# Hybrid Fourier / state-space encoder layer on one core: modulation matmuls turned round and half of them moved, weight sums queued behind weight loads, one norm moved into the MLP

## Chip, cores and metric

One core of a Trainium2 chip runs the whole layer as one program. The metric is the device time of one execution in microseconds; the lower, the better. Everything is computed in 32-bit floats.

## The reference, cut to what matters

One encoder layer for two requests (2048 and 512 tokens of width 1024; here side by side as 2560 tokens, features on the partitions).

```python
mod = silu(c) @ w_ada + b_ada                  # 1024 -> 6*1024, one row for each request
shift1, scale1, gate1, shift2, scale2, gate2 = split(mod, 6)
h  = rmsnorm(x, g_mix_norm) * (1 + scale1) + shift1
z  = h @ w_in
yf = fourier_mixer(z[..., :512])               # 2-D DFT, then a map for each head
ys = s5_mixer(z[..., 512:])                    # complex diagonal state space, both directions, GELU, GLU
x  = x + gate1 * (concat(rmsnorm(yf), rmsnorm(ys)) @ w_out)
h  = rmsnorm(x, g_mlp_norm) * (1 + scale2) + shift2
x  = x + gate2 * (square(relu(h @ w_mlp_in + b_in)) @ w_mlp_out + b_out)
y  = rmsnorm(x, g_final)
```

## The kernel before, in words

The program is straight-line code. A scheduler in the framework orders the instructions of each engine and each DMA queue when the program is built: an instruction is placed when it is ready in the scheduler's model, and of several that are ready the one written first goes first. At run time every engine and every queue keeps that order. SyncE (SP) only issues DMAs; ScalarE (ACT) and GpSimd (POOL) issue some between their own instructions. Most matmuls multiply split operands: `mm3` (L228 to 231) does three products, high by high, high by low, low by high, one pass each in fp32r. Plain fp32 matmuls take two records each in the trace.

Four stages follow each other, with some overlap.

1. **Input projection** (`mix_in`, to about 340 us). `ada1` makes the first 16 of the 48 modulation blocks of 128 columns (`mod[:, 0:16]`, shift1 and scale1) with the weights as the moving operand, 512 columns at a time (L705), then turns the result round with small transposes (L710). Beside the projection `zs` of five token tiles, `ssm_pre` (from about 55 to 177 us) builds the input and shift matrices of the state space, 8 groups `q`, at a raised priority and with its own three PSUM banks (`self.side = True`, L882). After each group it calls `ada_slot` twice (L290), but in the kernel before `ada_open(pre, A1)` with `A1 = 16` leaves these calls with nothing to do.
2. **State space beside Fourier mixing** (from about 340 to 690 us). For 8 groups `q`, `Ssm.lead` (psV matmuls, L350), `step1`, `step2`, `step3` (V sweeps on DVE, L403 to 417; psY matmuls, L382). Between these steps `slot` (L959) does one modulation block and one unit of the Fourier generator (`fourier`, then `out_f`, whose matmuls are `pof`). There are 32 such slots, two in each of the first two and last two rounds of the loop and four in each of the six between, so the 32 modulation blocks 16 to 47 are spread over the stage. A block is `ada(j)` (L681): eight fp32 matmuls with a 128x128 piece of the weights as the stationary operand and the two columns of `cs` as the moving one, then one DVE add (L688). Its weights (512 KB) are loaded by SP two blocks ahead (`AB = 2` buffers).
3. **Second half of the mixer** (`mix_out`, from about 690 to 1050 us). For five blocks `b` of 512 tokens: `gelu`, `glu`, and `out`, the output projection with the residual (`pout`), which stores the new x to `x1D`, sums its squares into `ss`, makes the row scales with `rbc` (matmuls `pn` L736, a power on POOL L750, matmuls `pb` L754, a copy on ACT L755) and stores them to `rD`. The MLP uses a Strassen-like scheme with seven products, for which sums of the weight quadrants are needed; `precombine` (L1247) loads four 256 KB quadrant pieces (SP, L1258), makes four sums on POOL (L1263) and stores them (ACT, L1264). Of 32 such pieces 20 are made here, with one buffer for each of `q0` to `q3`.
4. **MLP** (`mlp`, from about 1020 us to the end at 2663 us). Three blocks of tokens; each has 112 steps with `pf` matmuls and 112 with `acc` matmuls, twelve matmuls a step. Every second step SP loads a pair of weight tiles (`raw`, L1394, three buffers), ACT rounds them (L1404), DVE takes the rest (L1406), and in the first block SP stores that rest (L1408). `hooks` holds what else is called at a step: among them `pre2` for the last 12 `precombine` pieces at steps 4 to 55, with three sets of scratch inside one large tile `big` (L1507 to 1512), whose memory is shared with tiles of `mix_out`. Rows of `rD` are read by `rload`; those of the last 512 tokens are read only by the third token block.

Of the kernel before, what the change touches and what calls it, by code (L numbers as in the profile page):

```python
# [9 lines left out]
F32 = mybir.dt.float32  # L10
F32R = mybir.dt.float32r
# [6 lines left out]
LP, LS = 2048, 512  # L18
# [8 lines left out]
AB = 2  # L27
A1 = 16
YF = 2
# [203 lines left out]
def ssm_pre(net, P, pm, side, A, sI, sT, job):  # L233
# [5 lines left out]
    with tc.tile_pool(name="pre1", bufs=1, side=side) as tm, tc.tile_pool(name="pre2", bufs=1, side=side) as tp:  # L239
# [11 lines left out]
        for q in range(32 // NQ):  # L251
# [50 lines left out]
            for i in range(2):  # L302
                nc.scalar.dma_start(sT[q - 1 + i], Th[:, i * NQ:i * NQ + NQ].rearrange("p g h t -> p g (h t)"))


# [254 lines left out]
class Net:  # L560
# [3 lines left out]
    def run(self):  # L564
        tc, nc, A = self.tc, self.nc, self.A
        with ExitStack() as es:
# [25 lines left out]
            self.Ze = [fe.tile([96, n], F32R, name="Ze%d" % n) for n in (352, 256)]  # L592
            self.aj, self.wa = 16, {}
            self.pcs = [(w, c) for w in range(2) for c in range(16)]
# [8 lines left out]
            for q in range(nb + 2):  # L603
                if q < nb:
                    bl.append(S.lead(q))
                    self.slot(gen)
                if 1 <= q <= nb:
                    S.step2(bl[q - 1])
                if q >= 2:
                    self.slot(gen)  # L610
                    S.step3(bl[q - 2])
                    self.slot(gen)
                if q < nb:
                    S.step1(bl[q])
                    self.slot(gen)
            self.pull(gen, 1000)
            self.banks(7)
# [63 lines left out]
    def ada(self, j):  # L681
        nc = self.nc
        v3 = lambda n: self.v[n].unsqueeze(2).broadcast_to([128, 8, 2])
        ps = self.ps([128, 2], "pa")
        w = self.wa.pop(j)
        for k in range(8):
            nc.tensor.matmul(ps, w[:, k], self.cs[:, k], start=k == 0, stop=k == 7)  # L687
        nc.vector.tensor_scalar(self.mod[:, j], ps, self.v["b_ada"][:, j:j + 1], None, op0=ALU.add)  # L688
        if j == 39:
            nc.vector.scalar_tensor_tensor(self.gs2, self.mod[:, 32:40], 1.0, v3("g_mlp_norm"), op0=ALU.add, op1=ALU.mult)  # L690
        if j == 47:
            nc.vector.tensor_scalar(self.ng2, self.mod[:, 40:48], -1.0, None, op0=ALU.mult)
            nc.vector.tensor_tensor(self.gb2, self.mod[:, 40:48], v3("b_mlp_out"), op=ALU.mult)
# [277 lines left out]
    def fourier(self):  # L971
# [5 lines left out]
        with ExitStack() as es:  # L977
# [7 lines left out]
            part = lambda n: tt.tile([128, 516], F32, tag="zin", name="zin", bufs=2)[:, :n]  # L985
            zz = t0.tile([128, 94], F32, name="zz")
            v.memset(zz, 0.0)
            for z in Z:
                nc.scalar.copy(z[:, :, 258:352], bc(zz.unsqueeze(1), [128, 4, 94]))
            lines = [self.fourier_line(tt, tp, CW, CW3, L, ts, Z if L == LP else [t0.tile([128, 1, 352], F32R, name="Zs%d" % x) for x in range(2)], part, zz) for L, ts in self.SEQ]  # L990
            def maps():
# [22 lines left out]

    def fourier_line(self, tt, tp, CW, CW3, L, ts, Z, part, zz):
        nc, A = self.nc, self.A
# [3 lines left out]
        T = lambda n, sh, bufs=1, pool=tp: pool.tile(sh, F32R, tag=tag + n, name=n, bufs=bufs)  # L1020
        if L != LP:
            for z in Z:
                nc.scalar.copy(z[:, 0, 258:352], zz)
# [133 lines left out]
    def mix_out(self):  # L1157
        tc, nc, A = self.tc, self.nc, self.A
        v = nc.vector
        with ExitStack() as es:  # L1160
# [49 lines left out]
            def out(b, mg):  # L1210
                s = slice(b * TB, (b + 1) * TB)
                bb = b // 4
                ss = to.tile([128, TB], F32, name="ss")
                for m in range(8):
# [13 lines left out]
                    if m:  # L1228
                        v.tensor_tensor(ss, ss, q, op=ALU.add)
                nc.scalar.dma_start(self.rD[:, s], self.rbc(to, ss, 8, TB))  # L1230
            g = gelu(0)
            prev = None
            for b in range(5):
                mg = glu(g)
                if prev:
                    out(*prev)
                if b < 4:
                    g = gelu(b + 1)
                    for c in range(PCG):
                        if c % 4 == b:  # L1240
                            self.precombine(tp, 1)
                prev = (b, mg)
            tgs.close()
            self.mw = self.mws.enter_context(R("mw"))
            out(*prev)

# [19 lines left out]
    def mlp(self):  # L1266
# [12 lines left out]
        with tc.tile_pool(name="mp1", bufs=1, side="right") as t1, tc.tile_pool(name="mp", bufs=1, side="right") as tp:  # L1279
# [110 lines left out]
            def raw(i):  # L1390
                st = steps[i]
                w = A["w%d" % st["ph"]] if st["kind"] == "raw" else self.wS[st["ph"] - 1]
                raws[i] = mw.tile([128, 2, 512], F32, tag="wr", name="wr", bufs=3)
                nc.sync.dma_start(raws[i].rearrange("p a b -> p (a b)"), w[st["j"], st["m"] // 2])  # L1394
                los[i] = mw.tile([128, 2, 512], F32R, tag="wl", name="wl", bufs=3)
# [60 lines left out]
            def mm_out(st):  # L1456
# [8 lines left out]
                if k == SW - 1:  # L1465
                    for d in range(4):
                        for q in to[pi]:
                            dd, half = d + 4 * (q[0] == "2"), int(q[1]) - 1
                            for c0, c1, bb in segs(bl, half):
                                o = bl["xa"][:, 8 * half + dd, c0:c1]  # L1470
                                g = (self.ng2 if pi == 4 else self.mod[:, 40:48])[:, dd, bb:bb + 1]
                                v.scalar_tensor_tensor(o, acc[d][:, c0:c1], g, o, op0=ALU.mult, op1=ALU.add)

            steps, hooks = [], {}
            at = lambda i, f, *a: hooks.setdefault(i, []).append((f, a))
# [31 lines left out]
            def pre2(c):  # L1507
                if c == 0:
                    bl = blocks[0]
                    bl["sc"] = big(bl, "21").rearrange("p a b -> p (a b)")  # L1510
                t = blocks[0]["sc"]
                self.precombine(lambda n, i: t[:, 512 * (i + 4 * (c % 3)):512 * (i + 4 * (c % 3)) + 512])
            for c in range(len(self.pcs)):
# [35 lines left out]
```

## Time and profile before

| what | value |
|---|---|
| median of 3 runs | 2664.16 us (2652.8 to 2665.39) |
| profiled execution, its own time | 2665.03 us |
| span of the profiled execution | 2663.3 us |
| mean granted TensorE clock | 0.954 of 2.4 GHz |
| TensorE (PE) busy | 2530.6 us, 95% of the span |
| VectorE (DVE), ScalarE (ACT), GpSimd (POOL) busy | 1683.9, 1293.1, 478.7 us |
| DMA | 627.31 MB, mean 236 GB/s |

A busy PE is not a PE at its best: its records overlap, and at the lower of its two clocks (1.2 GHz, shown as 0.50) the same matmuls take twice as long. So a stage is read by three numbers together: the busy time, the granted clock and the busy time of the engines beside it.

### The profile page before, as it was taken

Reading aid. Unit: us, or ns where it says so; the run is one execution under the profiler, and the core shown is the slowest. Engines: PE = TensorE matmul, PEld = TensorE weight load, DVE = VectorE, ACT = ScalarE, POOL = GpSimd, SP = SyncE. Lnnn points to the kernel's source line nnn. Section 1 sums busy time; section 2 is a strip of 40 time slices with the busy share of each in tenths; the row PEclk is TensorE's granted clock in tenths of the full one; section 3 lists DMA queues with packets and bytes.
Section 4 is the critical chain, followed back from the end, with each engine's and each line's share of the span. In section 5 each row is a group of like instructions: output and inputs, shape, how many; then the busy total and the mean of one; then the engine's idle time right before and its main releaser. Section 6 shows DMA issues by size and latency. Waiting matters only on the chain.

```text
span 2663.3 us, 35333 instructions
## 1 busy us (share of the span) xinstructions
PE 2530.6 (95%) x12643; PEld 2285.1 (86%) x12643; DVE 1683.9 (63%) x2775; ACT 1293.1 (49%) x2267; POOL 478.7 (18%) x406
## 2 busy tenths in 40 slices
PE   6889999999989999799999999999999999999997
PEld 2778878778767779689999999999999999999997
DVE  7888778776638866758867973354456433634454
ACT  2643466564534425525544557355445573654443
POOL 4410010000346430940400002004000020130000
PEclk8789988879999999899999999999999999999998
DMA  8644476455678978997666777676667766766664
GB/s 293 205 146 113 141 246 214 163 171 184 206 274 268 308 253 288 339 365 277 233 218 216 276 257 251 228 273 230 226 230 276 248 243 226 274 226 227 226 222 163
DMA packets 279040, 627.31 MB, mean 236 GB/s; under 512 B 66512, under 2 KB 110608, under 8 KB 277072
## 3 DMA queue, kind: packets, MB, share of 16 engines
q1 hardware_dynamic: 238416, 549.13, 60.3%
q10 hardware_dynamic: 34096, 61.32, 6.2%
q0 software_dynamic: 6352, 14.60, 1.7%
q8 instruction: 100, 1.64, 0.3%
q14 instruction: 76, 0.62, 0.1%
HBM read 469.10 MB, written 155.85 MB: 235 GB/s over the span
## 4 chain that ended last, share of the span: by engine, by line
PE 68%; DVE 12%; DMA 10%; ACT 4%; issue 4%; POOL 2%; ACTq 0%; SPq 0%; DVEq 0%; POOLq 0%
PE acc L231 9%; PE acc L230 9%; PE acc L229 9%; PE pf L231 8%; PE pf L230 8%; PE pf L229 8%; PE pa L687 2%; PE psY L382 2%; PE psV L350 1%; DMA xq<-in_xq 1%; POOL q L1263 1%; DMA wS<-q 1%; DMA q<-in_w 1%; DVE wl L1406 1%; PE pof L229 1%
## 5 line engine op out<-in xcount | busy, mean ns | idle before, releaser
L1404 ACT CAST wh<-wr 128x512 fp32r<-128x512 f32 x672 | 413.4, 620 | 689.3 <-PE acc L230 342.7
L229 PE MATMUL pf<-th,wh 128*128 128x426 f32 (+1 forms) x1344 | 483.2, 360 | 19.7 <-ACT wh L1404 19.6
L230 PE MATMUL pf<-th,wh 128*128 128x426 f32 (+1 forms) x1344 | 482.2, 359 | 1.0 <-DVE th L1357 1.0
L231 PE MATMUL pf<-th,wl 128*128 128x426 f32 (+1 forms) x1344 | 477.3, 359 | 5.2 <-DVE wl L1406 5.1
L230 PE MATMUL acc<-th,wh 128*128 128x426 f32 (+1 forms) x1344 | 478.4, 357 | 0.3 <-DVE th L1357 0.3
L229 PE MATMUL acc<-th,wh 128*128 128x426 f32 (+1 forms) x1344 | 474.5, 357 | 0.0
L231 PE MATMUL acc<-th,wl 128*128 128x426 f32 (+1 forms) x1344 | 466.9, 357 | 2.1 <-DVE wl L1406 2.0
L1424 DVE TENSOR_TENSOR big<-big,pf 128x426 f32<-128x426 f32 (+1 forms) x320 | 185.1, 596 | 237.2 <-PE pf L231 191.6
L1357 DVE TENSOR_TENSOR th<-big,th 128x1704 fp32r<-128x1704 f32 (+1 forms) x82 | 158.8, 1936 | 201.8 <-ACT th L1356 201.5
L229 PEld LDWEIGHTS pf<-th,wh 128*128 128x128 f32 x1344 | 254.3, 189 | 32.8 <-ACT wh L1404 23.4
L231 PEld LDWEIGHTS pf<-th,wl 128*128 128x128 f32 x1344 | 254.3, 189 | 18.0 <-DVE wl L1406 9.1
L230 PEld LDWEIGHTS pf<-th,wh 128*128 128x128 f32 x1344 | 254.7, 190 | 10.1 <-DVE th L1357 1.4
L231 PEld LDWEIGHTS acc<-th,wl 128*128 128x128 f32 x1344 | 253.2, 189 | 11.2 <-DVE wl L1406 2.8
L230 PEld LDWEIGHTS acc<-th,wh 128*128 128x128 f32 x1344 | 252.5, 188 | 9.5 <-DVE th L1357 1.1
L229 PEld LDWEIGHTS acc<-th,wh 128*128 128x128 f32 x1344 | 252.9, 188 | 9.0
L750 POOL TENSOR_TENSOR r<-r,mh 128x4 f32<-128x4 f32 (+3 forms) x32 | 35.3, 1109 | 1145.1 <-DVE r L749 1145.1
L1431 POOL TENSOR_TENSOR big<-big 128x426 f32<-128x426 f32 (+1 forms) x128 | 142.6, 1118 | 493.4 <-ACT big L1430 490.1
L1406 DVE TENSOR_TENSOR wl<-wr,wh 128x512 fp32r<-128x512 f32 x224 | 174.9, 799 | 62.6 <-ACT wh L1404 62.1
L1263 POOL TENSOR_TENSOR q<-q,q 128x512 f32<-128x512 f32 x80 | 138.4, 1730 | 79.6 <-DMA q<-in_w 57.4
L1356 ACT CAST th<-big 128x1704 fp32r<-128x1704 f32 (+1 forms) x82 | 132.5, 1616 | 0.7 <-PE acc L231 0.7
L1357 DVE TENSOR_TENSOR th<-x,th 128x1704 fp32r<-128x1704 f32 (+1 forms) x23 | 47.5, 2066 | 69.3 <-ACT th L1356 69.3
L1430 ACT ACTIVATE big<-big 128x426 f32<-128x426 f32 (+1 forms) x128 | 71.3, 559 | 38.7 <-DVE big L1424 35.5
(444 smaller groups left out, 4453.4 us busy)
## 6 DMA issues: line engine op xcount, KB each, us to landing
wl<-wL SPq DMA_DIRECT2D x224, 512.0 KB, 3.5
wr<-wS SPq DMA_DIRECT2D x192, 512.0 KB, 4.5
wr<-in_w SPq DMA_DIRECT2D x144, 512.0 KB, 4.4
wL<-wl SPq DMA_DIRECT2D x112, 512.0 KB, 3.4
wa<-in_w_ada SPq DMA_DIRECT2D x48, 512.0 KB, 4.7
q<-in_w SPq DMA_DIRECT2D x80, 256.0 KB, 4.3
wS<-q ACTq DMA_DIRECT2D x80, 256.0 KB, 3.7
big<-x1D SPq DMA_DIRECT2D x8, 1704.0 KB, 7.8
```

The costliest lines, as they stand in the source:

```text
L229: nc.tensor.matmul(out, l[0], r[0], start=start, stop=False)
L230: nc.tensor.matmul(out, l[0], r[1], start=False, stop=False)
L231: nc.tensor.matmul(out, l[1], r[0], start=False, stop=stop)
L382: nc.tensor.matmul(py, m, x[:, j], start=i == 0, stop=i == 2)
L1263: e.tensor_tensor(o, x, y, op=op)
L1356: nc.scalar.copy(th[0], src)
L1357: return th, v.tensor_tensor(th[1], src, th[0].bitcast(F32), op=ALU.subtract)
L1404: nc.scalar.copy(hi, r)
L1406: v.tensor_tensor(lo, r, hi.bitcast(F32), op=ALU.subtract)
L1424: v.tensor_tensor(f[q], f[q], ps, op=op)
L1430: nc.scalar.activation(f[q], f[q], AF.Relu)
L1431: nc.gpsimd.tensor_tensor(f[q], f[q], f[q], op=ALU.mult)
```

## The change

The modulation blocks 16 to 47 are computed the other way round: `cs` (two columns) is stationary, the weights move, the result `[2, 128]` is copied by ACT to `ar` and turned to `[128, 2]` by a transpose one block later (`ada_turn`). `A1` becomes 32, so that 16 of the 32 blocks run in the slots of `ssm_pre`. The zeros for the Fourier tiles are no longer kept in a tile of their own. The scratch of `precombine` in `mix_out` gets two buffers for one. In the MLP the loads of `precombine` are ordered behind the newest weight load on SP (order only, no wait). The last block of `out` only sums the squares; the row scales of its 512 tokens are made in the MLP at steps 12 and 16, 256 tokens each.

```diff
-A1 = 16
+A1 = 32
@@ ssm_pre, after the loop over q
+        net.ada_turn()
@@ run
-            self.aj, self.wa = 16, {}
+            self.aj, self.wa, self.turn = 16, {}, None
...
+            self.ada_turn()
             self.pull(gen, 1000)
@@ ada
-        ps = self.ps([128, 2], "pa")
+        ps = self.ps([2, 128], "pa")
         w = self.wa.pop(j)
         for k in range(8):
-            nc.tensor.matmul(ps, w[:, k], self.cs[:, k], start=k == 0, stop=k == 7)
+            nc.tensor.matmul(ps, self.cs[:, k], w[:, k], start=k == 0, stop=k == 7)
+        self.ada_turn()
+        r = self.adp.tile([2, 128], F32, name="ar")
+        nc.scalar.copy(r, ps)
+        self.turn = (j, r)
+
+    def ada_turn(self):
+        nc = self.nc
+        if not self.turn:
+            return
+        (j, r), self.turn = self.turn, None
+        v3 = lambda n: self.v[n].unsqueeze(2).broadcast_to([128, 8, 2])
+        ps = self.ps([128, 2], "pat")
+        nc.tensor.transpose(ps, r, self.ident[:2, :2])
         nc.vector.tensor_scalar(self.mod[:, j], ps, self.v["b_ada"][:, j:j + 1], None, op0=ALU.add)
@@ fourier, fourier_line
-            zz = t0.tile([128, 94], F32, name="zz")
-            v.memset(zz, 0.0)
+            def zeros():
+                zz = part(94)
+                v.memset(zz, 0.0)
+                return zz
+            zz = zeros()
...
         if L != LP:
+            zz = zeros()
@@ mix_out, out and the loop over b
-                ss = to.tile([128, TB], F32, name="ss")
+                ss = to.tile([128, TB], F32, name="ss") if b < 4 else self.mw.tile([128, TB], F32, name="ss")
...
+                if b == 4:
+                    return ss
                 nc.scalar.dma_start(self.rD[:, s], self.rbc(to, ss, 8, TB))
...
-                            self.precombine(tp, 1)
+                            self.precombine(tp, 2)
...
-            out(*prev)
+            self.ssl = out(*prev)
@@ mlp
-                nc.sync.dma_start(raws[i].rearrange("p a b -> p (a b)"), w[st["j"], st["m"] // 2])
+                self.wload = nc.sync.dma_start(raws[i].rearrange("p a b -> p (a b)"), w[st["j"], st["m"] // 2])
...
+            def norm_last(h):
+                o = 256 * h
+                nc.scalar.dma_start(self.rD[:, NT - TB + o:NT - TB + o + 256], self.rbc(tp, self.ssl[:, o:o + 256], 8, 256))
...
-                self.precombine(lambda n, i: t[:, 512 * (i + 4 * (c % 3)):512 * (i + 4 * (c % 3)) + 512])
+                with tc.issue_after(self.wload.ins):
+                    self.precombine(lambda n, i: t[:, 512 * (i + 4 * (c % 3)):512 * (i + 4 * (c % 3)) + 512])
+            for h in range(2):
+                at(12 + 4 * h, norm_last, h)
```

## Rows read from the trace of the kernel before

**Rows 1.** The page, busy time of the engines: us, share of the span, instructions.
```profile
PE 2530.6 (95%) x12643; PEld 2285.1 (86%) x12643; DVE 1683.9 (63%) x2775; ACT 1293.1 (49%) x2267; POOL 478.7 (18%) x406
```

**Rows 2.** Windows by stage: length, busy PE, PEld, DVE, ACT, POOL; clock, DMA share, GB/s.
```profile
50.00:177.00 127.00, 103.49 (x540) 89.38 (x540) 109.98 (x190) 65.95 (x177) 49.52 (x39) 0.79 0.63 205
...
340.00:450.00 110.00, 108.64 (x574) 90.74 (x574) 100.09 (x278) 66.44 (x191) 7.03 (x12) 0.84 0.77 247
450.00:660.00 210.00, 202.91 (x952) 163.59 (x952) 154.27 (x409) 116.53 (x252) 4.32 (x5) 0.85 0.49 164
...
690.00:1000.00 310.00, 285.09 (x1249) 229.18 (x1249) 209.19 (x270) 122.24 (x192) 149.68 (x89) 0.96 0.80 266
...
1060.00:1190.00 130.00, 105.94 (x490) 94.83 (x489) 85.98 (x88) 54.70 (x96) 94.23 (x64) 0.92 0.97 356
...
1250.00:2600.00 1350.00, 1346.76 (x6937) 1300.11 (x6936) 734.89 (x931) 686.63 (x1052) 144.44 (x136) 1.00 0.69 241
```

**Rows 3.** Windows of the modulation instructions (tile pa) alone: PE, PEld, DVE, ACT.
```profile
340.00:450.00 110.00, 26.34 (x188) 26.81 (x188) 2.15 (x10) 0.00 (x0) 0.84 0.77 247
450.00:660.00 210.00, 44.71 (x324) 46.03 (x324) 4.75 (x22) 0.00 (x0) 0.85 0.49 164
...
536.00:538.00 2.00, 2.00 (x14) 2.00 (x13) 0.22 (x1) 0.00 (x0) 0.66 0.84 228
```

**Rows 4.** Windows of 2 us, two at a fall and two at a rise of the clock.
```profile
534.00:536.00 2.00, 2.00 (x21) 2.00 (x20) 2.00 (x5) 0.03 (x1) 0.00 (x0) 1.00 0.96 303
536.00:538.00 2.00, 2.00 (x15) 2.00 (x14) 1.97 (x6) 0.00 (x0) 0.00 (x0) 0.66 0.84 228
...
30.00:32.00 2.00, 2.00 (x4) 0.34 (x3) 2.00 (x14) 0.09 (x1) 0.00 (x0) 0.64 1.02 358
32.00:34.00 2.00, 2.00 (x6) 0.42 (x5) 2.00 (x12) 1.15 (x2) 0.00 (x0) 1.00 1.03 401
```

**Rows 5.** Windows of nine low-clock stretches, the first and the last.
```profile
377.00:386.00 9.00, 9.00 (x29) 6.79 (x29) 8.68 (x28) 4.83 (x16) 1.59 (x3) 0.50 1.04 312
...
643.00:649.00 6.00, 6.00 (x18) 4.63 (x19) 0.22 (x1) 0.64 (x2) 0.00 (x0) 0.50 0.51 172
```

**Rows 6.** Tile pa: count, duration ns min/median/max, first and last start, shapes.
```profile
L687 PE MATMUL pa<-cs,wa x512: 165/251/354, 345.3 to 656.3; 128*128 128x2 f32 x171
...
L705 PE MATMUL pa<-wa,cs x64: 591/592/1061, 5.8 to 48.6; 128*2 128x512 f32 x64
L688 DVE TENSOR_SCALAR mod<-pa,vec x32: 195/216/221, 348.8 to 656.6; 128x2 f32<-128x2 f32 x32
L707 ACT COPY ar<-pa x4: 558/572/576, 15.4 to 50.8; 2x512 f32<-2x512 f32 x4
```

**Rows 7.** Tile pat: the small transposes of the first 16 blocks.
```profile
L710 PE MATMUL pat<-ident,ar x16: 191/196/218, 16.1 to 51.7; 2*128 2x2 f32 x16
```

**Rows 8.** The page, DMA issues: count, KB each, median us to landing.
```profile
wa<-in_w_ada SPq DMA_DIRECT2D x48, 512.0 KB, 4.7
```

**Rows 9.** Waits of the SP queue, 690 to 1050 us: total us, times, longest.
```profile
SPq L1258 <- DMA wS<-q: 55.6, 37, 5.5
```

**Rows 10.** Timeline of the SP queue at the start of the MLP.
```profile
1049.30 0.39 SPq L1394 DMA_DIRECT2D wr<-in_w  x1
1056.99 6.70 SPq L1258 DMA_DIRECT2D big<-in_w  x12
...
1066.73 1.88 SPq L1394 DMA_DIRECT2D wr<-in_w  x2
```

**Rows 11.** Timeline of ACT: the last store of x and that of the last row scales.
```profile
1042.57 0.33 ACTq L1225 DMA_DIRECT2D x1D<-xo  x1
...
1052.51 0.33 ACTq L1230 DMA_DIRECT2D rD<-rb  x1
```

**Rows 12.** Waits from 1060 to 1120 us, the longest of PE.
```profile
PE pf L229 <- ACT wh L1404: 13.7, 2, 9.9
```

**Rows 13.** Timeline of POOL, the first sums in the MLP.
```profile
1063.73 16.97 POOL L1263 TENSOR_TENSOR big<-big 128x512 f32<-128x512 f32 x9 [14.73 <-DMA big<-in_w]
```

More of the change, by code (lines that the diff above doesn't have):

```diff
@@ L682, in ada @@
         nc = self.nc
-        v3 = lambda n: self.v[n].unsqueeze(2).broadcast_to([128, 8, 2])
-        ps = self.ps([128, 2], "pa")
+        ps = self.ps([2, 128], "pa")
         w = self.wa.pop(j)
         for k in range(8):
-            nc.tensor.matmul(ps, w[:, k], self.cs[:, k], start=k == 0, stop=k == 7)
+            nc.tensor.matmul(ps, self.cs[:, k], w[:, k], start=k == 0, stop=k == 7)
[11 more added lines that the diff above has]
+        nc.tensor.transpose(ps, r, self.ident[:2, :2])
         nc.vector.tensor_scalar(self.mod[:, j], ps, self.v["b_ada"][:, j:j + 1], None, op0=ALU.add)
@@ L985, in fourier @@
             part = lambda n: tt.tile([128, 516], F32, tag="zin", name="zin", bufs=2)[:, :n]
-            zz = t0.tile([128, 94], F32, name="zz")
-            v.memset(zz, 0.0)
+            def zeros():
[3 more added lines that the diff above has]
+            zz = zeros()
             for z in Z:
                 nc.scalar.copy(z[:, :, 258:352], bc(zz.unsqueeze(1), [128, 4, 94]))
-            lines = [self.fourier_line(tt, tp, CW, CW3, L, ts, Z if L == LP else [t0.tile([128, 1, 352], F32R, name="Zs%d" % x) for x in range(2)], part, zz) for L, ts in self.SEQ]
+            lines = [self.fourier_line(tt, tp, CW, CW3, L, ts, Z if L == LP else [t0.tile([128, 1, 352], F32R, name="Zs%d" % x) for x in range(2)], part, zeros) for L, ts in self.SEQ]
             def maps():
@@ L1013, in fourier, with fourier_line @@
                         lines.remove(g)
-    def fourier_line(self, tt, tp, CW, CW3, L, ts, Z, part, zz):
+    def fourier_line(self, tt, tp, CW, CW3, L, ts, Z, part, zeros):
         nc, A = self.nc, self.A
```

## Prediction

> **What bounds the kernel now.** I read the page first, then windows by stage, then what each stage waits for. PE is busy for 95% of the span [rows 1], but that figure hides two different situations. From 1250 to 2600 us PE is busy for 1346.8 of 1350 us at the full clock [rows 2]: the body of the MLP is PE's own work, and nothing in this change shortens it. Before that, three stages lose time in different ways [rows 2]. From 340 to 660 us PE is busy almost throughout, but its clock is 0.84 and 0.85: 110 x 0.16 + 210 x 0.15 = 49 us of full-speed work is missing there, while DVE has 10 us idle in the first window and 56 us in the second. From 690 to 1000 us PE is idle for 25 us at 0.96. From 1060 to 1190 us it is idle for 24 us at 0.92 while the DMA engines are 97% busy at 356 GB/s: that stretch waits for data. From 50 to 177 us DVE is the fuller engine (110 of 127 us) and PE has 23.5 us idle at 0.79.
>
> **Why the clock is low in the second stage.** The modulation blocks take 71.05 us of PE there [rows 3], in 512 records. From 534 to 536 us PE is busy without a gap at 2.4 GHz; in the next 2 us, all of it modulation records [rows 3], the clock falls to 1.2 GHz (0.66 is the mean of the two levels) though PE still has no gap [rows 4]. Nine low stretches of 4 to 10 us begin in or just after such a burst, and one minus the clock, times the length, adds up to 29.9 us over the nine; the first alone gives 9 x 0.50 = 4.5 us and the last 6 x 0.50 = 3.0 us [rows 5]. The other low stretches follow real idle time. The opposite form, weights moving, is already in the kernel for the first 16 blocks: there the clock rises from 1.2 to 2.4 GHz while PE does little else [rows 4], and stays up.
>
> The Trainium skill, page "TensorE: Matmul & The Clock Gate", section "What's actually happening", says that the slow clock is the default and that activity releases it; by that rule a gapless burst should not lower the clock, and turning the operands round would give none of the 29.9 us back. The row at 536 us speaks against it; it is rival B below.
>
> **Part 1: modulation.** Cost of a block in the new form. The shortest 512-column record takes 591 ns and the shortest 2-column record 165 ns [rows 6], so 510 columns add 426 ns and 128 columns cost 107 ns at 2.4 GHz, 214 at 1.2. A block has 8 matmuls of two records: 1.7 us, or 3.4. The old form takes 71.05 / 32 = 2.22 us on average, so the swap itself saves little. New are a transpose, two records of 196 ns, 0.4 us [rows 7]; a copy on ACT, under 572 ns for a quarter of the columns [rows 6]; the DVE add of 216 ns stays [rows 6]. The transpose comes one block later, so its copy is long done; if ACT is late, PE waits for that copy with everything behind it.
>
> *Taken out of the second stage:* 16 blocks, 16 x 2.22 = 35.5 us of PE; up to 29.9 us of clock from the nine stretches; against that 16 transposes, 6 us. So PE can give at most 59 us. DVE's room sets the other limit: 10 us up to 450 us, 56 us after [rows 2]. The state-space chain runs from psV over ACT copies and DVE sweeps to psY, so PE's relief will not all become time. I take half of the first room and 30 us of the second, 35 us together; bounds 5 (only the first half-room: the chain binds) and 59.
>
> *Put into 50 to 177 us:* 16 blocks at 1.7 + 0.4 = 34 us of PE, against 23.5 us idle: 10 us over. DVE gets 16 x 0.216 = 3.5 us, and has 17 idle. The 16 loads (512 KB, 4.7 us to landing [rows 8]) go on SP, where the `xn` loads of the next tile's norm stand behind a load that waits for its buffer, that is for PE to finish the block two before; the first two may go out at once and compete with the first stage's own loads. The blocks also share three PSUM banks with the state-space matrices, and the memory of that pool is needed by the folds that follow. I take a loss of 10 us; bounds 0 (all in PE's idle time; the clock of 0.79 is not counted as a gain) and 54 (16 x 3.4 at the slow clock, all serial).
>
> **Part 2: two buffers in `mix_out`.** SP waits 55.6 us in 37 pieces for a sum to be stored before it can reload the scratch [rows 9], and loads of y, x and pD's stores stand behind it. With two buffers most of that goes; the same bytes at a DMA share of 0.80 [rows 2] will then come earlier, possibly ahead of urgent loads. POOL's sums still hold up ACT's stores. Of 25 us PE idle I take 5 us back; bounds -5 and +12.
>
> **Part 3: sums behind weight loads, and the last norm.** At 1049.3 us SP issues a weight pair, then stands until 1057 us for the scratch; then twelve sum loads go out, and the next weight pair only at 1066.7 us [rows 10]. PE waits 13.7 us for weights [rows 12]. The scratch comes free when the row scales of the last block are stored (1052.5 us); the last store of x was issued at 1042.6 us [rows 11]. Without the norm the scratch is free about 8 to 10 us earlier. The order behind the newest weight load binds little: by the hooks at steps 4, 8 and 13 the first three pieces need four, six and nine pairs ahead of them, and the pair at 1049.3 us is already the tenth; by the same count only the last four or five of the 12 pieces are held back, by a pair or two. It moves no bytes away, and the stretch is full of DMA. Idle time and lost clock there are 24 + 130 x 0.08 = 34 us; I take 10 us back; bounds -10 and +25.
>
> The norm's matmuls are as many as before. Its power now runs on POOL at steps 12 and 16, where POOL has nine sums in 17 us after a 14.7 us wait for data [rows 13]; if it stands behind them, `pb` and all of PE's later matmuls wait. That is why Part 3 has a negative bound. The zeros add a memset: nothing, DVE's idle time hides it.
>
> **Sum.** 35 - 10 + 5 + 10 = 40 us. The profiled execution took 2665 us, 1 us above the median of the runs shown, so 2665 - 40 = 2625 us.
>
> **Rivals.** *A, the chain binds* (chance 0.15): the second stage is set by DVE sweeps and ACT copies, PE merely fills; it returns 5 instead of 35, 2655 us. For it: DVE at 100 of 110 us up to 450 us. Against it: 56 us of DVE idle time after that. *B, the clock does not come back* (0.12): PE's share of the gain then loses the 29.9 us; of 59 it keeps 29, half of it becomes time: 15 instead of 35, 2645 us. For it: some stretches follow idle time; against it: rows 4. *C, the new loads stop the first stage* (0.10): SP's loads of modulation weights wait for PE, `xn` waits behind them, and each of the 16 blocks costs its landing and its matmuls, 4.7 + 1.7 = 6.4 us, 102 us in all when nothing overlaps; against the 50 us returned elsewhere that is 2665 + 52 = 2717 us. At two thirds of it, 68 us, it is 2683 us. It decides from 50 us, 3.1 us a block. For it: two blocks stand together after each group with only two buffers. Against it: eight groups in 122 us are some 15 us apart, so a load has time to land. *D, the ordering does nothing and the sums still collide* (0.08): Part 3 gives 0, 2635 us. The forecast keeps 0.55.
>
> **How the numbers follow.** A measurement of this kernel can tell about 0.5%, 13 us, from no change: faster means under 2651 us. Forecast and D are nearly all faster, B mostly, A hardly half, C not: 0.54 + 0.08 + 0.09 + 0.06 = 0.77. Slower is most of C, 0.09; the rest, 0.14, is within. The range reaches down to 2588 us, where the second stage gives 59 and the sums 20 (59 - 10 + 8 + 20 = 77), and up to 2662 us, which takes in A; C is left out above.
>
> **What would show it.** Right: no fall of the clock after modulation records, 340 to 660 us shorter by some 35 us with a clock above 0.92, the state-space matrices ending before 190 us, the sum loads starting at once after the tenth weight pair, PE idle in that stretch under 18 us. Wrong: a clock still near 0.85, DVE full in the second stage, PE or SP standing for modulation weights before 177 us, or `pb` waiting for POOL in the MLP.

## The result, and the profile after

The changed kernel takes 2693.97 us (median of 4 runs, 2688.4 to 2698.51) against 2661.92 us for the kernel before in the same comparison (2652.8 to 2665.39): ratio 1.0125, 95% interval 1.0088 to 1.0162. It is slower by 32 us where 40 us less were forecast. Its profiled execution took 2689.43 us, with a span of 2687.7 us.

The busy times of the page, to compare with [rows 1], and the windows of the five stretches of [rows 2] shifted to where they now lie (length; busy PE, PEld, DVE, ACT, POOL; clock, DMA share, GB/s):

```profile
PE 2515.5 (94%) x12675; PEld 2243.9 (83%) x12675; DVE 1686.5 (63%) x2777; ACT 1299.8 (48%) x2300; POOL 465.7 (17%) x407
```

```profile
50.00:195.00 145.00, 127.46 (x812) 102.25 (x812) 92.85 (x177) 67.36 (x191) 42.73 (x39) 0.92 0.67 219
379.00:490.00 111.00, 97.48 (x532) 71.76 (x531) 86.32 (x241) 65.71 (x198) 10.93 (x18) 0.92 0.74 225
490.00:690.00 200.00, 179.10 (x822) 133.11 (x820) 166.87 (x434) 124.36 (x277) 6.63 (x5) 0.94 0.44 146
712.00:1030.00 318.00, 287.57 (x1254) 232.12 (x1253) 229.90 (x285) 129.07 (x199) 146.05 (x89) 0.94 0.81 272
1092.00:1222.00 130.00, 111.35 (x527) 99.27 (x526) 83.74 (x93) 55.79 (x100) 78.15 (x57) 0.96 0.92 335
```

PE is busy for 15 us less than before and the clock of the second stage is up from 0.84 and 0.85 to 0.92 and 0.94. Yet the program is longer. Four marks, read from the first start of a tile's matmuls, divide the span: **I** (first stage) up to the first psV, **II** (second stage) from there to the first pgate, **III** (second half of the mixer) to the first pf, **IV** (MLP) to the end.

| | I | II | III | IV |
|---|---|---|---|---|
| before | 331.9 | 430.0 | 257.8 | 1643.6 |
| after | 379.1 | 404.2 | 268.4 | 1636.0 |
| difference | +47.2 | -25.8 | +10.6 | -7.6 |

The four add up to the 24.4 us between the two spans. The second stage gained, by less than the 35 us forecast; the first stage lost far more than forecast, and the second half of the mixer lost instead of gaining. The 7.6 us of the MLP say nothing: among the kernels whose MLP is that of before (the kernel before and, below, e1_pad, e8_no_part3, e9_q2_alone, e10_pad_mix and e13_q2_no3) IV lies anywhere from 1639.2 to 1650.3 us.

**Where the first stage lost.** It has two parts: up to the start of the last psT matmul of the state-space matrices (173.4 us before, 192.6 after: +19.2), and the time from there to the first psV (158.5 us before, 186.5 after: +28). The second is not the matrices. The weights of the folds (`we`, made from `rawf` over `wf`) were made beside the matrices before. Rows of tile `we`, first the kernel before (duration, first and last start):

```profile
L225 ACT CAST we<-wf x8: 602/620/623, 77.1 to 146.4; 128x514 fp32r<-128x514 f32 x8
```

and the kernel after, from the view of tile wf:

```profile
L913 DVE TENSOR_TENSOR wf<-rawf x8: 408/415/432, 77.3 to 231.0; 128x255 f32<-128x255 f32 x8
L225 ACT CAST we<-wf x8: 619/621/624, 188.1 to 231.4; 128x514 fp32r<-128x514 f32 x8
```

The first `wf` is ready at 78 us, as before, but its copy to `we` starts at 188.1 us, released by a store of `It` (timeline of ACT after; in brackets the idle time before and what ended it):

```profile
183.02 0.81 ACTq L275 DMA_DIRECT2D s<-It  x2
...
188.06 0.62 ACT L225 CAST we<-wf 128x514 fp32r<-128x514 f32 x1 [2.75 <-DMA s<-It]
```

`It` is scratch of the matrices and has nothing to do with the folds. What they have in common is memory. In the built programs, `we0` and `we1` occupy bytes 58464 to 91360 of a partition in both kernels. The scratch pool of the matrices (`pre2`: CC, I, cb, It, M, Dm) began at byte 96384 before. The two weight buffers (2 x 4096) and `ar` (512) of the moved blocks are in the pool that is laid out before it and push it down by 8704 bytes, to 87680, so 3680 bytes are now shared. `we0` ends at byte 74912 and shares no byte, and yet its first copy (188.1 us) waits for the scratch as well: in this program the order is kept pool by pool. SP's row shows the same, the last five `rawf` loads (three of the eight went out at 52 to 78 us):

```profile
190.31 16.71 SPq L909 DMA_DIRECT2D rawf<-in_w_in  x5
```

### The profile page after: what moved, and what is told of

It reads as the page before. It is cut to its first block, busy times and chain, and to the rows that moved or that the text cites. A ratio compares the mean times of both kernels' runs of the same rounds, so it can differ in the third digit from the quotient of the medians.

```text
span 2687.7 us, 35469 instructions
## 1 busy us (share of the span) xinstructions
PE 2515.5 (94%) x12675; PEld 2243.9 (83%) x12675; DVE 1686.5 (63%) x2777; ACT 1299.8 (48%) x2300; POOL 465.7 (17%) x407
## 4 chain that ended last, share of the span: by engine, by line
PE 68%; DMA 11%; DVE 11%; ACT 5%; issue 3%; POOL 2%; SPq 1%; ACTq 0%; DVEq 0%; POOLq 0%
PE acc L230 9%; PE acc L231 9%; PE acc L229 9%; PE pf L231 8%; PE pf L229 8%; PE pf L230 8%; DMA xn<-in_xn 2%; DMA q<-in_w 1%; POOL q L1284 1%; PE psY L383 1%; PE pa L688 1%; DVE wl L1427 1%; PE ps L229 1%; PE ps L231 1%; PE ps L230 1%
## 5 line engine op out<-in xcount | busy, mean ns | idle before, releaser
L229 PEld LDWEIGHTS pf<-th,wh 128*128 128x128 f32 x1344 | 253.7, 189 | 26.6 <-ACT wh L1425 17.3
L231 PEld LDWEIGHTS pf<-th,wl 128*128 128x128 f32 x1344 | 253.7, 189 | 19.2 <-DVE wl L1427 10.3
L765 POOL TENSOR_TENSOR r<-r,mh 128x4 f32<-128x4 f32 (+4 forms) x33 | 36.6, 1114 | 1099.9 <-DVE r L764 1085.3
```

The lines of the kernel that those rows point to most:

```text
L229: nc.tensor.matmul(out, l[0], r[0], start=start, stop=False)
L231: nc.tensor.matmul(out, l[1], r[0], start=False, stop=stop)
L765: nc.gpsimd.tensor_tensor(r[:m, js], r[:m, js], self.mh[:m, js], op=ALU.pow)
```

## Experiments

Ratios are to runs of the kernel before in the same comparison (medians of before 2660 to 2664 us); the stages are from one profile of each, and "psT ends" is the start of the last psT matmul. In the eight kernels with the first stage of before, I lies between 330.1 and 334.6 us and psT ends between 170.8 and 174.5, so differences of that size mean nothing.

| run | median us | ratio, 95% interval | psT ends | I | II | III | IV |
|---|---|---|---|---|---|---|---|
| e1_pad | 2696.33 | 1.0134, 1.0097 to 1.0170 | 177.7 | 367.3 | 412.9 | 261.3 | 1650.3 |
| e2_one_wa | 2699.18 | 1.0151, 1.0127 to 1.0174 | 212.3 | 381.4 | 389.9 | 280.6 | 1639.4 |
| e3_late | 2678.03 | 1.0071, 1.0056 to 1.0086 | 174.5 | 331.7 | 415.3 | 292.9 | 1636.0 |
| e4_q1 | 2681.62 | 1.0080, 1.0058 to 1.0102 | 191.9 | 377.9 | 395.4 | 257.2 | 1641.0 |
| e5_late_q1 | 2652.26 | 0.9964, 0.9951 to 0.9977 | 172.1 | 330.1 | 408.2 | 268.6 | 1644.4 |
| e6_room | 2653.80 | 0.9975, 0.9964 to 0.9986 | 193.5 | 356.0 | 391.3 | 264.4 | 1639.4 |
| e7_eight | 2641.74 | 0.9932, 0.9914 to 0.9949 | 177.2 | 336.7 | 398.5 | 260.8 | 1644.9 |
| e8_no_part3 | 2651.84 | 0.9962, 0.9948 to 0.9976 | 173.1 | 334.6 | 410.4 | 265.1 | 1641.3 |
| e9_q2_alone | 2669.66 | 1.0017, 1.0003 to 1.0031 | 174.3 | 334.3 | 422.0 | 263.8 | 1650.2 |
| e10_pad_mix | 2658.99 | 0.9991, 0.9973 to 1.0009 | 172.0 | 330.9 | 426.9 | 255.6 | 1641.8 |
| e11_eighth | 2651.09 | 0.9946, 0.9929 to 0.9963 | 184.9 | 346.8 | 391.4 | 266.6 | 1642.7 |
| e12_spread | 2681.51 | 1.0062, 1.0046 to 1.0079 | 220.2 | 387.6 | 383.9 | 270.7 | 1639.7 |
| e13_q2_no3 | 2675.96 | 1.0048, 1.0031 to 1.0065 | 172.8 | 330.1 | 409.6 | 292.1 | 1639.2 |
| e14_late_pad | 2649.68 | 0.9959, 0.9941 to 0.9978 | 170.8 | 330.3 | 410.8 | 265.0 | 1642.1 |
| e15_no_loads | 2657.36 | 0.9985, 0.9968 to 1.0002 | 194.4 | 358.4 | 391.0 | 266.3 | 1637.6 |
| e16_neither | 2648.61 | 0.9945, 0.9920 to 0.9971 | 186.6 | 344.9 | 390.2 | 265.5 | 1643.1 |

### Is it the memory? e1_pad and e2_one_wa, then e6_room

```diff
 # e1_pad, on the kernel before
             self.ada_open(pre, A1)
+            pad = pre.tile([128, 2176], F32, name="pad")
+            v.memset(pad[:, 0:1], 0.0)
```

> The kernel before, with 8.5 KB per partition more in the pool `pre` that nothing uses, so that the scratch of the state-space matrices starts at byte 87680 as in the changed kernel and no longer at 96384; the folded weights `we` end at byte 91360. No block is moved, and no matmul, load or add of the modulation is changed. Theory M (memory: the folded weights now share bytes with that scratch, so the folding waits until the scratch is closed): the first `we` is made at about 180 us in place of 77, the first psV matmul comes at 360 to 380 us in place of 332, and the whole time rises by 28 to 48 us, to 2690 to 2710 us. Rival W (the work of the 16 blocks on TensorE, VectorE and SyncE makes the first stage longer): nothing changes, first psV at 330 to 335 us, 2655 to 2670 us.

Measured: as theory M says. Eight and a half unused kilobytes make the kernel before slower by 36 us. The matrices end 4.3 us later, I is 35.4 us longer. Its `we` row:

```profile
L225 ACT CAST we<-wf x8: 604/622/622, 171.6 to 218.3; 128x514 fp32r<-128x514 f32 x8
```

```diff
 # e2_one_wa, on the kernel after (ada_open and ada_slot)
+        self.ab = 1 if end == A1 else AB     # used where AB stood
```

> The changed kernel with one buffer in place of two for the modulation weights while the state-space matrices are built. The scratch then starts at byte 91776, just above the folded weights (91360); all 16 blocks stay where the change put them. Theory M: the folding runs beside the matrices again (first `we` at about 80 us), the first psV matmul comes at 335 to 352 us in place of 379, and the time falls by 27 to 44 us against the changed kernel, to 2650 to 2667 us. Rival W: each block now also waits for its own load, first psV at 379 us or later, 2694 to 2715 us.

Measured: both theories half right. `we` is early again (80.8 us), but I is no shorter, because the matrices now end at 212.3 us. PE stands for the weights of about every second block (its waits from 55 to 215 us; total, times, longest):

```profile
PE pa L688 <- DMA wa<-in_w_ada: 18.5, 7, 4.2
```

So one wait was traded for another, and the clash had to be removed with both buffers in place:

```diff
 # e6_room, on e4_q1
-                    r = hp.tile([128, 512], F32, name="rawf", bufs=2)
+                    r = hp.tile([128, 512], F32, name="rawf", bufs=1)
-CB = 2
+CB = 1
 # and bufs=1 for M and Dm (CB is the number of CC sets)
```

> As the run before with one buffer for the sums, and all 16 blocks with two buffers beside the state-space matrices as the change has them, but with 3.75 KB freed in that pool and its neighbour (rawf 2 buffers to 1, M and Dm 2 to 1, the CC set 2 to 1), so that the scratch starts at byte 91520, above the folded weights. Theory M (memory): the first `we` is made at 75 to 85 us, the first psV comes at 335 to 352 us in place of 378, the second stage keeps its 395 us, time 2632 to 2655 us. Rival W (the work of the blocks in the first stage is what costs, and a start of the folding before the matrices are done does not help): first psV at 365 us or later, time 2670 to 2685 us.

Measured: `we` at 74.9 us, and against e4_q1, which it differs from in nothing else, I falls by 21.9 us and the time by 28 us, to 2653.80 us. The time from the last psT to the first psV is back at 162.5 us. But psT still ends at 193.5 us and the first psV comes 24 us later than before the change, outside of what M said. That rest is what the blocks and their room cost. The two parts overlap, so the 47.2 us can't be divided once for all: the memory clash alone makes I 35.4 us longer (e1_pad) and the blocks add 11.8 to that; without the clash the blocks cost 24.1 us and the clash adds the rest. And the room was made by halving buffers in the matrices' own scratch (CC, M, Dm); no run has these smaller buffers without the blocks, so a part of the 24 us may be theirs (from 55 to 195 us ACT waits 6.6 us for the one CC set in e16_neither, and 3.1 us for the two in the kernel before).

### What is the blocks' own part? e11, e15, e16, and e7, e12

```diff
 # e11_eighth, on e6_room
-        for k in range(8):
+        n = 1 if j < A1 else 8
+        for k in range(n):
 # e15_no_loads, on e6_room (e16_neither: both)
-        w = self.wa.pop(j)
+        w = self.wa[16 + j % 2] if j < A1 else self.wa.pop(j)
```

> The kernel with room for both buffers and all 16 blocks beside the state-space matrices, but each of these 16 blocks makes one of its eight products (7/8 of their matrices' products are left out; all loads, copies, transposes and adds stay). Theory T (what is left of the first stage's loss is TensorE's own work, 1.9 us a block, put between the steps of the matrices): psT ends 16 x 1.65 = 26 us earlier at the most, so at 172 to 180 us in place of 193.5, and the first psV comes at 333 to 343 us in place of 356. Rival L (it is the loads on SP or the copies on ScalarE): psT ends at 188 us or later, first psV at 350 to 356 us.

> The kernel with room for both buffers and 16 blocks beside the state-space matrices, where these 16 blocks use the weights of the first two over and over: 14 loads of 512 KB are left out, every product, copy, transpose and add stays. If the loads are what is left of the first stage's loss (SP's queue and the DMA engines): psT ends at 175 to 183 us in place of 193.5, first psV at 335 to 345 us in place of 356. If it is the work on TensorE and the steps around it: psT ends at 188 to 194 us, first psV at 350 to 357 us.

> The same with one of eight products in each of these 16 blocks as well, so that neither the loads nor 7/8 of the products are there; copies, transposes and adds stay. If loads and products together are what is left: psT ends at 173 to 178 us, first psV at 332 to 338 us, as before the change. If the steps around them (copy on ScalarE, transpose one block later, the shared PSUM banks) hold up the matrices: psT ends at 180 to 186 us, first psV at 341 to 347 us, as with the loads and without the products.

Measured: without the loads nothing changes (psT 194.4, I 358.4). Without 7/8 of the products psT ends 8.6 us earlier, without both 6.9 us, where up to 26 us of PE work went away. The windows up to the end of the matrices in e11_eighth say why it may be so little; in order e6_room, e11_eighth, e15_no_loads and e16_neither:

```profile
150.00:185.00 35.00, 34.10 (x252) 28.56 (x253) 11.96 (x36) 14.56 (x47) 3.66 (x5) 1.00 0.63 210
```

```profile
150.00:185.00 35.00, 30.80 (x150) 27.46 (x148) 21.08 (x46) 13.59 (x44) 5.97 (x8) 0.54 0.67 226
```

```profile
150.00:185.00 35.00, 35.00 (x244) 28.83 (x243) 15.09 (x38) 10.71 (x35) 5.55 (x6) 1.00 0.32 101
```

```profile
150.00:185.00 35.00, 30.86 (x150) 26.86 (x149) 20.08 (x48) 11.04 (x36) 7.54 (x7) 0.58 0.28 101
```

The DMA share falls from 0.63 to 0.32 without the loads, and the matrices are no faster. With their products the clock is 1.00, without them 0.54 and 0.58, near the lower level, and the matrices' own matmuls take longer (median psT record 275 ns with, 370 ns without). 35 us at 0.46 less is 16 us of full-speed work, an estimate of what leaving the products out took from the matrices again. That it held up their end by so much is argued, not shown: no run leaves the products out and keeps the clock up, and in kernels without moved blocks a lower clock there cost no time that shows (from 150 to 172 us it is 1.00 in e8_no_part3 and 0.83 in e10_pad_mix, and psT ends at 173.1 and 172.0 us). So the runs show that the products cost some 9 us and the loads none; how much the lost clock hides is open. What is left without products and loads, 13 us, was not taken apart: copies, transposes, adds, the shared PSUM banks and the smaller scratch buffers remain as rivals. 5 us of it stand at the start, where the first pst waits until 61.5 us in place of 56.7.

```diff
 # e7_eight, on e2_one_wa with one buffer for the sums
-A1 = 32
+A1 = 24
-            for _ in range(2):
-                net.ada_slot()
+            net.ada_slot()
```

> One buffer for the sums; 8 blocks, one after each group, with one buffer, beside the state-space matrices (no clash of memory: the scratch starts at byte 91776), the other 24 in the second stage. A load has a whole group, some 15 us, to land. Theory M: psT ends at 176 to 185 us, first psV at 333 to 343 us, second stage 398 to 410 us, time 2630 to 2648 us. Rival W (any block there holds up the matrices by its own load and matmuls, 16 blocks with one buffer gave psT an end at 212 us against 173): psT ends at 190 us or later, first psV at 355 us, time over 2655 us.

Measured: as theory M says in every stage; 2641.74 us, the best of all, 0.68% under the kernel before. The eight blocks cost the first stage some 5 us (I is 336.7 us, against 330.1 to 334.6 without them), and the second is 9.7 us shorter than with all blocks in it (e5_late_q1).

```diff
 # e12_spread: all 16 blocks, one weight buffer, on e4_q1's sums
+            net.ada_slot()                   # right behind the psm matmuls
             M = T("M", [128, 2, NQ, 16])
 ...
-            for _ in range(2):
-                net.ada_slot()
+            net.ada_slot()
```

> One buffer for the sums; all 16 blocks beside the state-space matrices with one buffer for their weights (no clash of memory), one block right behind the psm matmuls of a group and one at its end, so that each load has about half a group, 7 us, to land. If loads that land late were what held the matrices up with one buffer (psT at 212 us): psT ends at 180 to 190 us, first psV at 340 to 352 us, second stage 388 to 396 us, time 2636 to 2650 us. If it is the blocks' matmuls: psT ends at 193 to 200 us, first psV at 355 to 362 us, time 2650 to 2662 us, no better than with 8 blocks (2642 us).

Measured: neither. psT ends at 220.2 us, worse than with the blocks in pairs, and PE still waits 16.7 us for the loads, against 18.5 in pairs: half a group did not cover a load that may only start when the block before has been read. Why the matrices end even later than in pairs was not taken apart.

### The second buffer of the sums: e4_q1, e3 with e5, e9, e10, e13, e14

```diff
 # e4_q1, on the kernel after
-                            self.precombine(tp, 2)
+                            self.precombine(tp, 1)
 # e3_late, on the kernel after; e5_late_q1: both edits
-A1 = 32
+A1 = 16
```

> The changed kernel with one buffer for each of the four pieces of a sum in the second half of the mixer, as before. If the second buffer made that stage longer: the first pgate to the last pout comes back from 268 us to 255 to 260 us and the time falls by 6 to 13 us, to 2681 to 2688 us. If the 10 us come from the new order of the last block (its squares kept for the MLP) or from where the stage begins: 266 to 270 us and no change, 2689 to 2699 us. As forecast, that the second buffer helps: the stage gets longer still, over 270 us.

> The changed kernel with all 32 blocks in the slots of the second stage (A1 = 16), in the new form. Both theories give the first stage back (first psV at 330 to 336 us). What it tells is what the form alone is worth in the second stage, from the first psV to the first pgate: 430 us before, 404 us in the changed kernel. If the form brought the clock back, 408 to 422 us and a clock above 0.93 there, time 2650 to 2668 us; if the gain came from taking 16 blocks away, 425 to 435 us and 2668 to 2685 us.

> The changed kernel with all 32 blocks in the second stage and with one buffer for each of the four pieces of a sum. Theory (the memory clash and the second buffer are what costs, the new form itself gains): first psV at 330 to 336 us, first psV to first pgate 405 to 416 us, from there to the MLP 255 to 262 us, time 2632 to 2650 us, faster than both kernels. Rival (the state-space chain takes back what PE gains): second stage 425 to 432 us, time 2650 to 2662 us.

Measured: with one buffer III is 257.2 us again and the time 12 us less; on the kernel with all blocks late it is 26 us. e3_late's total, 2678.03 us, lies in the range of its second expectation, but its II (415.3 us) is that of the first: III, at 292.9 us, made up the difference. e5_late_q1 has I and II as its theory said, but III is 268.6 us against 255 to 262 at most, so that its 2652.26 us miss the 2650 us and fall in the rival's range of times; the rival's II of 425 us or more did not occur.

```diff
 # e9_q2_alone, on the kernel before
-                            self.precombine(tp, 1)
+                            self.precombine(tp, 2)
 # e10_pad_mix on the kernel before, e14_late_pad on e5_late_q1
+            pad = tp.tile([128, 2048], F32, name="pad")
+            v.memset(pad[:, 0:1], 0.0)
             g = gelu(0)
 # e13_q2_no3: e8_no_part3 (below) with the second buffer
```

> The kernel before with the second part of the change alone: two buffers for each of the four pieces of a sum in the second half of the mixer. Theory S (the second buffer costs: SP's loads for sums go out earlier and in between the loads of x and y, so that blocks of the output projection come later): first pgate to the MLP 265 to 285 us against 257.8, time 2670 to 2690 us. The forecast (it gains 5 us): 250 to 256 us, 2652 to 2660 us. If it only costs together with the new form of the blocks: no change, 2657 to 2667 us.

> The kernel before with 8 KB per partition more in the pool of the second half of the mixer that nothing uses, as much as the second buffers take; the loads stay as they are. Theory S (order of the loads): no change, first pgate to the MLP 255 to 261 us, 2655 to 2667 us. Rival P (memory again: the larger pool shares bytes with something that then has to wait): 265 to 285 us and 2670 to 2690 us, as with the second buffers.

> All 32 blocks late in the new form, two buffers for the sums, the third part undone (norm of the last block in the mixer, no order for the sums in the MLP). With the third part this was 2678 us, with one buffer and without the third part 2652 us. If the second buffer costs by itself beside the new form: 2670 to 2682 us, first pgate to the MLP 280 to 295 us. If it costs only together with the third part: 2652 to 2660 us, 262 to 270 us.

> All 32 blocks late, one buffer for the sums, the third part kept, and 8 KB per partition in the mixer's pool that nothing uses, where the second buffers would be. Without those 8 KB it was 2652 us, with them used as second buffers 2678 us. Theory S (order and time of the loads): 2648 to 2657 us, first pgate to the MLP 258 to 270 us. Rival P (memory shared with something that has to wait): 2668 to 2682 us, 280 to 295 us.

Measured: it is not memory this time (e10 and e14: no change), nor the third part (e13: 24 us without it). The second buffer costs in each of four pairs: 12, 26 and 24 us by the medians beside the new blocks, but in the kernel before only 4.5 us by its ratio, short of what theory S said and barely clear of nothing (the interval goes from 0.8 to 8 us). What it does is in the rows of SP's loads; first the kernel before, then after (count, duration, first and last start):

```profile
L1258 SPq DMA_DIRECT2D q<-in_w x80: 327/370/999, 680.3 to 972.8; - x80
```

```profile
L1279 SPq DMA_DIRECT2D q<-in_w x80: 327/423/1701, 712.3 to 943.1; - x80
L1235 SPq DMA_DIRECT2D xo<-in_xT x40: 327/333/1536, 817.0 to 1054.5; - x40
```

and in what SP waited for from 712 to 1030 us after, to set beside [rows 9]:

```profile
SPq L1237 <- DVE xo L1239: 69.3, 26, 5.7
...
SPq L1279 <- DMA wS<-q: 13.9, 9, 5.2
```

SP's wait for the stores fell from 55.6 to 13.9 us, as forecast, and the 80 loads are all out 160 us after the first pgate in place of 211. But none of them is needed before the MLP, and in SP's order they now stand between the loads of y, x and pD. From the last x1D store of the first output block to that of the second it is 73 us in e13_q2_no3 (848.9 to 922.1) and 48 us in e8_no_part3 (848.1 to 896.5), the same with one buffer. After the change, PE waits for `mg` once, for 7.3 us. That the order of the loads does this is argued from the rows and not shown. It is not that the DMA engines are full: in those two stretches their share is 0.77 with the second buffer and 0.89 without. And the scheduler orders every engine anew when the buffers change: PE runs 280 matmul records in the first of the two stretches and 209 in the second. No run changes the order of SP's loads alone. Why the kernel before suffers less wasn't found out.

### The third part: e8_no_part3

```diff
 # on e5_late_q1
-                if b == 4:
-                    return ss
-                with tc.issue_after(self.wload.ins):
-            for h in range(2):
-                at(12 + 4 * h, norm_last, h)
```

> The kernel of the first run of this call (all 32 blocks late, one buffer for the sums) with the third part of the change undone: the sums in the MLP are not ordered behind the weight loads, and the last norm stands in the mixer again. Theory (part 3 gains some 5 to 10 us, as forecast): MLP from the first pf to the end 1642 to 1648 us against 1634 to 1641 us with it, time 4 to 12 us over that run. Rival (part 3 does nothing, what it moves is hidden or falls on a stretch full of DMA either way): within 3 us of it.

Measured: 2651.84 us without the part, 2652.26 us with it: no difference. This is also the run of the new block form alone, 0.9962 of the kernel before. The loads of the sums did start earlier with the part, 26 us after the first pf (1033.4 against 1006.9 us) in place of 35 (1045.1 against 1010.1). But the last of the 48 goes out at the same time; with the part (e5_late_q1), then without:

```profile
L1279 SPq DMA_DIRECT2D big<-in_w x48: 327/454/1051, 1033.4 to 1165.9; - x48
```

```profile
L1277 SPq DMA_DIRECT2D big<-in_w x48: 327/446/1213, 1045.1 to 1165.4; - x48
```

From the first of these loads to 1166 us the DMA engines are busy for 0.95 of the time with the part and for 0.97 without: in a stretch as full as this the loads that started sooner ended no sooner.

## Why the prediction was wrong

**The step that failed** is "Put into 50 to 177 us: ... I take a loss of 10 us". It measured 47.2 us, inside its bounds of 0 to 54 and far from the value taken. (With that bound of 54 in the sum the forecast would be 2669 us; the range ended at 2662, so it did not hold what the prediction itself thought possible.) The larger cause is memory, by which the folding of weights waits for the matrices: 35 us when it acts alone (e1_pad), 22 us on top of the blocks (e6_room against e4_q1). The prediction wrote that "the memory of that pool is needed by the folds that follow" and gave it no price: it asked who needs that memory next, not what lies beside it already. With the clash gone the blocks and their room still cost 24 us. The cost of a block on PE was nearly right (after the change 34.44 us for the 16 blocks' records, 2.15 us each, plus 0.22 for the transpose, against 1.7 + 0.4), and the mistake was to set 34 us of it against 23.5 us of PE idle time as if all of that were free room. Leaving out 7/8 of the products gave back only 9 us; the rest of the 24 is open, as said above.

**Second stage, 35 us gained:** 25.8 us measured, and part of that may come with a later start: e1_pad, in which no block changed, has a II shorter by 17 us. The mechanism held: without moving a block (e8_no_part3, e5_late_q1) the clock is up. The windows of e5_late_q1, against 0.84 and 0.85 in [rows 2]:

```profile
340.00:450.00 110.00, 104.03 (x577) 76.50 (x578) 93.66 (x260) 67.11 (x199) 6.16 (x10) 0.95 0.73 226
450.00:660.00 210.00, 200.58 (x1051) 145.08 (x1049) 160.38 (x428) 125.21 (x282) 6.20 (x5) 1.00 0.54 182
```

Of 49 us of missing full-speed work all but 5.5 (110 x 0.05) came back, more than the 29.9 us taken from the nine stretches. It became 20 to 22 us of II, of which III took back 7 to 11; 10 us are left in the median of e8_no_part3.

**Second buffers, 5 us gained:** 12 us lost (after against e4_q1), a wrong sign and outside the bounds of 5 us lost and 12 gained. The words "will then come earlier, possibly ahead of urgent loads" named the mechanism that the rows suggest, and gave it too little weight.

**Third part, 10 us gained:** nothing measurable. That PE idles there while DMA is 97% busy was read correctly, and so was "It moves no bytes away"; the step from there to 10 us back had no row behind it.

**The rivals.** A (the chain binds) is part of the truth: regained PE time became time by half. B fell: the clock came back. C had the right total, 2683 to 2717 us, by luck: its mechanism did not occur, since without 14 of the 16 loads the stage is as long (e15_no_loads against e6_room). D was right about the third part.

Nothing here overturns the Trainium skill's rule (page "TensorE: Matmul & The Clock Gate", section "What's actually happening") that activity releases the throttle. Runs e11 and e16 agree with it, with a clock of 0.54 and 0.58 with fewer products against 1.00 in both runs with all of them. What did not follow from it is how little the old form's gapless records held up the clock [rows 4].

## What to carry to other kernels

Before moving work into another stage, compute the bytes its buffers take there and see what else lies at the addresses that shift: a pool pushed 3.7 KB too far serialised two parts of the kernel that share no data, and an unused tile of the same size in the old kernel shows that in one run. Idle time of an engine inside a chain of short dependent steps is not simply room for more work: here eight blocks cost 5 us, and sixteen, with smaller scratch, 24. More buffers for work that is not urgent can cost time: here 4 to 26 us, perhaps because that work then passes work that is urgent.

## What the runs showed of the hardware that was not expected

Taking work away lowered the clock of what remained: with 7/8 of the products of 16 blocks left out, PE's busy time from 150 to 185 us fell only from 34.10 to 30.80 us, but its granted clock from 1.00 to 0.54. An experiment that leaves out matmuls to measure their cost therefore measures two things at once, and here it can't tell them apart.

An elementwise sum on DVE also takes longer while POOL adds. Two rows of DVE in the kernel after, the first inside POOL's sums of 926.35 to 931.04 us, the second in a gap between them:

```profile
928.12 1.77 DVE L1248 TENSOR_TENSOR ss<-ss,sq 128x512 f32<-128x512 f32 x1
...
937.69 0.69 DVE L1248 TENSOR_TENSOR ss<-ss,sq 128x512 f32<-128x512 f32 x1 [0.41 <-ACT sq L1246]
```

The same operation on the same shape takes 1.77 and 0.69 us. Of its 35 records four take longer than 0.9 us after the change, and each of them runs while POOL makes a sum; the others stay between 0.67 and 0.69. This is a rival for the second buffer's cost, in part: DVE is busy for 210.7 us of III after and for 197.4 us with one buffer (e4_q1). The row above does not account for it, since with one buffer nine of the 35 are slow; the second product in `gelu` does more (L1207, up to 1.78 us after and 0.91 with one buffer), and SP's loads of y wait for that line: 26.6 us after and 16.0 in e4_q1 (712 to 1030 us), 37.3 in e13_q2_no3 and 9.8 in e8_no_part3 (740 to 1030 us). How much of the second buffer's cost this is wasn't tried.
